# Down projection of a feed-forward layer by seven block products

## The chip, the core and the metric

One core of a Trainium2 chip runs the whole program. It has five engines with queues of their own: TensorE (PE, matmuls into PSUM; PEld is its weight load), VectorE (DVE), ScalarE (ACT), GpSimd (POOL, which does not touch PSUM here) and SyncE (SP), whose queue issues nearly all DMAs. The metric is the device time of one execution in microseconds, as the median of several.

## The reference, cut to what matters

One layer on 1024 rows of width 1024: an input projection, three groups of token mixers, an output projection with a layer norm, and then the part of this change:

```python
gu = jnp.einsum('bsd,df->bsf', x, w_gu)
gate, up = gu[..., :FFN_HIDDEN], gu[..., FFN_HIDDEN:]
ffn = jnp.einsum('bsf,fd->bsd', jax.nn.silu(gate) * up, w_down)
return layer_norm(DEEPNORM_ALPHA * x + ffn, ln2_g, ln2_b)
```

with FFN_HIDDEN = 2816, that is 22 chunks of 128, all in float32.

## The kernel before

Float32 accuracy on TensorE is had by splitting. An operand r is copied to h in the reduced format (`A.activation(h, r, AF.Copy)`, ScalarE), its rest is l = r - h (`sub(eng, l, r, f(h))`, line 158), and `mm3` (lines 180 to 182) adds the three products hh, hl, lh of 128x128 by 128x512 into one PSUM bank. The program is laid out by a planner: it orders each engine's instructions by its own forecast and puts tiles on the memory that is free, where `bufs` is the number of tiles of one tag that live at a time. So an instruction can be ahead of its place in the text, but on an engine they run strictly in the planned order. `tc.issue_after(i)` keeps a DMA behind instruction i on its queue.

*Up stage.* For each of the 22 chunks c the gate and up weights are loaded by `raws` (two tiles of tag raw, 512 KB each). Chunk 0 and 1 go plainly (`up_plain`, NPLAIN = 2); from chunk 2 on `up_strassen` uses seven products in place of eight for its own 2x2 blocks (84 matmuls): GpSimd makes four sums and differences of weight blocks (128x512 each, lines 1017 and 158), ScalarE and VectorE split them, VectorE puts the products together from PSUM and multiplies with the gate. `combos` makes the sums of the activation blocks once, while chunk 1 runs. The result th (128 hidden units by 1024 rows, of tag p with five buffers) goes to the DRAM tile `hd[c // 2][:, c % 2]` by one DMA of 512 KB in `put` (line 985), whose instruction `lead` serves later as a mark on SP's queue.

*Down stage.* Two halves hh of 512 rows, each with eight accumulators (four row tiles by two halves of the 1024 output columns), which fill all of PSUM. For each chunk `down_in` loads hidden units for 512 rows (a pair of chunks at a time) and 128 rows of `w_down`, and splits both (`split4`); `down_mm` then does 8 x 3 matmuls. The last six chunks (LASTN) are done row tile by row tile, so that the tiles end one after the other. Then VectorE adds the accumulator to 2 ALPHA x (line 1119), `layer_norm` works the statistics, and its second part scales: in mode dve on VectorE alone, in mode mix with half the columns on ScalarE and GpSimd. Each half tile is stored as it is done.

Names that matter below: `put`, `hidden`, `up_strassen`, `down_in`, `down_mm`, `layer_norm`, and the tiles th, hd, raw, y, psd.

## Time and profile before

| | us |
|---|---|
| median of three runs | 1423.05 (1419.74 to 1425.28) |
| the profiled execution | 1420.1 |
| its span in the trace | 1418.3 |
| TensorE busy in the span | 1329.7 (94%) |
| VectorE busy | 927.0 (65%) |
| ScalarE busy | 557.6 (39%) |
| GpSimd busy | 318.3 (22%) |

Busy time is a mean over stages that differ. In the first half, with attention and the selection of keys, TensorE has gaps; from about 790 us on, in the up and down stage, it has none. The busy time of a matmul in a row (0.39 us) is its latency, since matmuls are pipelined; what it costs is the distance from start to start. In a timeline row the number after the start is how long the instruction took with all that held it once it had begun, and in brackets stands how long its engine was idle before, and what ended that.

### The profile page before, as it was taken

How to read it: one execution, taken by the hardware profiler on the slowest of the kernel's cores; microseconds unless marked ns; L12 is line 12 of the kernel's file. 1: busy time of each engine (PE TensorE's matmuls, PEld its weight loads, DVE VectorE, ACT ScalarE, POOL GpSimd, SP SyncE). 2: the span in 40 equal slices, each digit the busy share in tenths (PEclk: the TensorE clock that was granted, in tenths of full speed). 3: DMA queues.
4: the chain of work that ended last, by engine and by line, in shares of the span. 5: the costliest groups of instructions: out<-in, count | busy, mean ns of one | idle time of the engine just before them, and what ended most of it. 6: DMA issues, size and time to landing. Idle time of an engine off the chain costs nothing.

```text
span 1418.3 us, 17526 instructions
## 1 busy us (share of the span) xinstructions
PE 1329.7 (94%) x6444; PEld 1065.8 (75%) x6444; DVE 927.0 (65%) x1821; ACT 557.6 (39%) x1033; POOL 318.3 (22%) x250
## 2 busy tenths in 40 slices
PE   7568987988999999899999999999999999999997
PEld 6457665676787886557788888888888888888886
DVE  5137899797657968444859776676667655348325
ACT  4145565666785534243313322222222233213310
POOL 1203221103132144400215333233333210000003
PEclk9779998899999999889999999999999999999999
DMA  6221111101111111315402222222222248427501
GB/s 192 76 74 59 49 29 43 36 9 38 51 40 41 50 34 49 96 51 182 149 33 91 86 74 90 89 79 85 90 77 75 87 182 336 149 89 269 206 0 60
DMA packets 107685, 127.46 MB, mean 90 GB/s; under 512 B 8144, under 2 KB 80720, under 8 KB 107600
## 3 DMA queue, kind: packets, MB, share of 16 engines
q1 hardware_dynamic: 106448, 122.15, 26.4%
q10 hardware_dynamic: 1152, 4.19, 0.8%
q8 instruction: 51, 0.84, 0.3%
q14 instruction: 34, 0.28, 0.1%
HBM read 97.49 MB, written 25.69 MB: 87 GB/s over the span
## 4 chain that ended last, share of the span: by engine, by line
PE 51%; DVE 1%; DMA 0%; issue 0%; ACT 0%; DVEq 0%; ACTq 0%; SPq 0%
PE p L181 9%; PE p L182 9%; PE p L180 9%; PE psd L180 6%; PE psd L182 6%; PE psd L181 6%; PE psz L182 1%; PE psz L180 1%; PE psz L181 1%; PE pg L180 1%; PE pu L182 1%; PE pu L180 1%; PE pg L182 1%; PE pg L181 1%; PE pu L181 1%; PE pst L208 0%
## 5 line engine op out<-in xcount | busy, mean ns | idle before, releaser
L559 ACT ACTIVATE junk<-sc_all,cf_a 128x768 bf16<-128x768 f32 (+2 forms) x93 | 96.7, 1039 | 35.9 <-DVE cf_a L553 14.1
L182 PE MATMUL psn<-hi_n,xTl 128*128 128x256 f32 x320 | 99.0, 309 | 0.0
L180 PE MATMUL psn<-hi_n,xTh 128*128 128x256 f32 x320 | 97.5, 305 | 0.9 <-DVE nm L664 0.9
L181 PE MATMUL psn<-lo_n,xTh 128*128 128x256 f32 x320 | 96.8, 302 | 0.0
L666 ACT ACTIVATE pt<-pt,nm 128x128 f32<-128x128 f32 (+7 forms) x96 | 74.0, 772 | 49.4 <-DVE nm L664 47.0
L198 POOL TENSOR_TENSOR lrs<-rv,mhalf 128x1 f32<-128x1 f32 x16 | 20.6, 1286 | 307.5 <-DVE rv L195 307.5
L1017 POOL TENSOR_TENSOR s<-raw_u 128x512 f32<-128x512 f32 x20 | 27.9, 1396 | 242.4 <-DMA raw_u<-in_w_gu_dram 206.9
L180 PEld LDWEIGHTS psn<-hi_n,xTh 128*128 128x128 f32 x320 | 66.2, 207 | 4.2 <-issue 2.0
L182 PEld LDWEIGHTS psn<-hi_n,xTl 128*128 128x128 f32 x320 | 66.2, 207 | 4.2 <-issue 3.0
L181 PEld LDWEIGHTS psn<-lo_n,xTh 128*128 128x128 f32 x320 | 65.8, 206 | 3.2 <-issue 1.6
L180 PE MATMUL p<-x1Th,gh 128*128 128x512 f32 x160 | 62.2, 389 | 0.0
L181 PE MATMUL p<-x1Tl,gh 128*128 128x512 f32 x160 | 62.2, 389 | 0.0
L182 PE MATMUL p<-x1Th,gl 128*128 128x512 f32 x160 | 62.2, 389 | 0.0
L365 PE MATMUL psi<-kst,qst 128*128 128x512 f32 (+1 forms) x80 | 29.0, 398 | 32.5 <-DMA qst<-qd 21.3
L372 DVE SCALAR_TENSOR_TENSOR sc_all<-rl,iw,sc_all 128x384 f32<-128x384 f32 (+5 forms) x42 | 41.4, 1046 | 27.5 <-ACT rl L367 27.4
L1043 DVE TENSOR_TENSOR th<-p,tp 128x512 f32<-128x512 f32 x20 | 13.8, 692 | 69.1 <-DMA hd<-th 57.6
L1059 ACT ACTIVATE sg<-tp 128x512 f32<-128x512 f32 x20 | 12.7, 634 | 105.6 <-DVE tp L1058 105.6
L664 DVE CUSTOM_DVE_ANT_0 pt<-psq,dist 128x512 f32<-128x512 f32 (+3 forms) x72 | 38.8, 546 | 22.0 <-PE psq L660 21.7
L198 POOL TENSOR_TENSOR rs<-rv,mhalf 128x1 f32<-128x1 f32 x32 | 19.1, 597 | 134.5 <-DVE rv L197 79.4
L1040 ACT ACTIVATE tp<-p 128x512 f32<-128x512 f32 x20 | 12.0, 600 | 93.6 <-DVE th L1065 80.4
L367 ACT ACTIVATE rl<-psi 128x512 f32<-128x512 f32 (+1 forms) x80 | 35.4, 562 | 23.7 <-PE psi L365 21.1
L682 PEld LDWEIGHTS pso<-vb,at 128*128 128x128 f32 x288 | 39.1, 206 | 7.0 <-DVE ob L705 2.4
(679 smaller groups left out, 4168.1 us busy)
## 6 DMA issues: line engine op xcount, KB each, us to landing
raw_g<-in_w_gu_dram SPq DMA_DIRECT2D x22, 512.0 KB
raw_u<-in_w_gu_dram SPq DMA_DIRECT2D x22, 512.0 KB
hd<-th SPq DMA_DIRECT2D x22, 512.0 KB
raw_n<-in_w_in_dram SPq DMA_DIRECT2D x10, 512.0 KB
x<-in_x_dram SPq DMA_DIRECT2D x8, 512.0 KB
raw_wo<-in_w_out_dram SPq DMA_DIRECT2D x8, 512.0 KB
mx<-mixd SPq DMA_DIRECT2D x8, 512.0 KB
y<-x1d SPq DMA_DIRECT2D x8, 512.0 KB
```

Source lines behind the costliest of these rows:

```text
L180: nc.tensor.matmul(ps, lh, rh, start=first, stop=False)
L181: nc.tensor.matmul(ps, lh, rl, start=False, stop=False)
L182: nc.tensor.matmul(ps, ll, rh, start=False, stop=last)
L198: GP.tensor_tensor(o, t, mhalf[:, 0:w], OP.pow)
L365: nc.tensor.matmul(ps[:, 0:w], qst[h][:, (i - 2) * P:(i - 1) * P], kst[:, o:o + w], start=True, stop=True)
L367: A.activation(r[:, o:o + w], ps[:, 0:w], AF.Relu)
L372: V.scalar_tensor_tensor(SC[i], r[:, 0:n], wcol, SC[i], op0=OP.mult, op1=OP.add)
L559: A.activation(junk_a[:, 0:P * (i + 1)], SC[i], AF.Sign, bias=f(cf)[:, j:j + 1], accum_out=cnt[:, j:j + 1])
L664: V.tensor_tensor_reduce(out=p[:, o:o + w], in0=ps[:, 0:w], in1=bias[:, o:o + w], scale=-slope, scalar=prev, op0=OP.add, op1=OP.min, accum ...
L666: A.activation(p[:, 0:n], p[:, 0:n], AF.Exp, bias=nm, scale=-1.0, accum_out=sm)
L682: nc.tensor.matmul(ps, at[:, j * P:(j + 1) * P], vsl(j0 + j), start=(j0 + j == 0), stop=(j0 + j == nk - 1))
L1017: GP.tensor_tensor(a[:, 0:4], u[:, 0:4], u[:, 4:8], OP.add)
```

## The change

Rows (two halves), hidden units (chunks j and j+11) and output columns (two halves) become the three pairs of blocks of a 2x2 by 2x2 product, which is done with seven products and sums before and after. Chunks are worked in the order 0, 11, 1, 12, ... For the first of a pair `put` keeps th (tag th, now two buffers) and stores its first half; for the second it stores th and four GpSimd results of 128x512, in two tiles of tag sh, with two more DMAs. So hd holds seven left operands per pair. The four blocks of `w_down` are loaded once each into 24 tiles (`wblock`), and GpSimd makes the differences of weights in place: t1 before product 3, one operation for each pair of chunks, t2 before product 4, three for each. A product goes over six pairs of chunks (the last a single chunk), with operands split in three buffers, into four accumulators; products alternate between the two sets of PSUM banks. Partial results stay in U, W and y, added by VectorE from PSUM and by GpSimd where both inputs are in SBUF. Seven of the eight norms are in mode mix; the first four stand in product 5, and the last product does its last three pairs row tile by row tile. The tag x8 has 13 buffers, and gl moves to the tag hi. The order of the products is 0, 1, 6, 3, 4, 5, 2.

```diff
     mixd = [dram.tile([P, DM], F32, name=f"mixd{i}") for i in range(NT)]
-    hd = [dram.tile([P, 2, S], F32, name=f"hd{i}") for i in range(NF // 2)]
+    NJ = NF // 2
+    hd = [dram.tile([P, 2, 7, 512], F32, name=f"hd{i}") for i in range((NJ + 1) // 2)]
     x1d = [dram.tile([P, DM], F32, name=f"x1d{i}") for i in range(NT)]
 
     sc_all = tl("sc", 1, "sc_all", (P, 4224))
...
         V.scalar_tensor_tensor(zz, zz, ALPHA, ps, op0=OP.mult, op1=OP.add)
 
     def x8(name, dt=F32R):
-        return pool.tile([P, 4, 512], dt, tag="x8", bufs=15, name=name)
+        return pool.tile([P, 4, 512], dt, tag="x8", bufs=13, name=name)
 
     def finish1(t):
         run(layer_norm(zs[t], g1t, b1t, EPS, "dve"))
...
     def w4(name, tag="st", bufs=11):
         return tl(tag, bufs, name, (P, KC, P), F32R)
 
+    first = {}
+
     def hidden(c):
-        return pp(f"th{c}")
+        return tl("th", 2, f"th{c}")
 
     def put(c, th):
-        return nc.sync.dma_start(hd[c // 2][:, c % 2], th).ins
+        if c < NJ:
+            first[c] = th
+            return nc.sync.dma_start(hd[c // 2][:, c % 2, 0], th[:, 0:512]).ins
+        j = c - NJ
+        d, a = hd[j // 2][:, j % 2], first.pop(j)
+        lead = nc.sync.dma_start(d[:, 1:3].rearrange("p a b -> p (a b)"), th).ins
+        u, v = tl("sh", 2, f"sa{j}"), tl("sh", 2, f"sb{j}")
+        a0, a1, b0, b1 = a[:, 0:512], a[:, 512:1024], th[:, 0:512], th[:, 512:1024]
+        GP.tensor_tensor(u[:, 0:512], a1, b1, OP.add)
+        sub(GP, u[:, 512:1024], u[:, 0:512], a0)
+        nc.sync.dma_start(d[:, 3:5].rearrange("p a b -> p (a b)"), u)
+        sub(GP, v[:, 0:512], a0, a1)
+        sub(GP, v[:, 512:1024], b0, u[:, 512:1024])
+        nc.sync.dma_start(d[:, 5:7].rearrange("p a b -> p (a b)"), v)
+        return lead
 
     def raws(c):
         r = []
...
         sub(GP, a[:, 4:8], a[:, 0:4], g[:, 0:4])
         sub(GP, b[:, 0:4], g[:, 0:4], u[:, 0:4])
         sub(GP, b[:, 4:8], g[:, 4:8], a[:, 4:8])
-        w = {"g": pair("g", g, V, w4(f"gh{c}", "hi", 3), w4(f"gl{c}", "lo", 3))}
+        w = {"g": pair("g", g, V, w4(f"gh{c}", "hi", 3), w4(f"gl{c}", "hi", 3))}
         for n, t in (("s12", a), ("s34", b)):
             w[n] = pair(n, t, V, w4(f"{n}h{c}"), w4(f"{n}l{c}"))
         uu = w4(f"uu{c}")
...
         V.tensor_tensor(h0, h0, t0, OP.mult)
         return put(c, th)
 
-    for c in range(NF):
-        if c == 1 or NPLAIN == 0 and c == 0:
+    leads = []
+    for n in range(NF):
+        c = n // 2 + n % 2 * NJ
+        if n == min(1, NPLAIN):
             T = combos()
...
+        leads.append((up_plain if n < NPLAIN else up_strassen)(c))
+
+    PAIRS = [(2 * p, min(2, NJ - 2 * p)) for p in range((NJ + 1) // 2)]
+    B = {}
+    srl = [leads[-3]]
+
+    def wblock(blk, r, d):
+        with tc.issue_after(srl[-1]):
+            for p, (j, w) in enumerate(PAIRS):
+                t = pool.tile([P, 1024], F32, tag="wd", bufs=24, name=f"B{blk}_{p}")
+                B[blk, p] = t[:, 0:512 * w].rearrange("p (a b) -> p a b", a=w)
+                src = wdn[(r + j) * P:(r + j + w) * P, d * 512:d * 512 + 512]
+                nc.sync.dma_start(B[blk, p], src.rearrange("(a p) d -> p a d", p=P))
+
+    wblock(11, 0, 0)
+
+    def split2(name, r, w):
+        h, l = (pool.tile([P, 2, 512], F32R, tag=f"{name}{e}", bufs=3, name=f"{name}{e}")[:, 0:w] for e in "hl")
         A.activation(h, r, AF.Copy)
-        sub(eng, l, r, f(h))
+        sub(V, l, r, f(h))
         return h, l
 
...
+    def operands(i, blk, p):
+        j, w = PAIRS[p]
+        r = pool.tile([P, 2, 512], F32, tag="sr", bufs=3, name="sr")[:, 0:w]
+        srl.append(nc.sync.dma_start(r, hd[p][:, 0:w, i]).ins)
+        return split2("S", r, w), split2("W", B[blk, p], w)
+
+    def product(i, blk, banks, prep, last=0):
+        acc = [al("psd") for al in banks]
+        ops = {}
+
+        def run_mm(p, t):
+            (sh, sl), (th, tl2) = ops[p]
+            j, w = PAIRS[p]
+            o = slice(t * P, t * P + P)
+            for q in range(w):
+                mm3(acc[t], sh[:, q, o], sl[:, q, o], th[:, q], tl2[:, q], j + q == 0, j + q == NJ - 1)
+
+        n = len(PAIRS)
+        for p in range(n - last):
+            prep(p)
+            ops[p] = operands(i, blk, p)
+            for t in range(4):
+                run_mm(p, t)
+        for p in range(n - last, n):
+            prep(p)
+            ops[p] = operands(i, blk, p)
+        for t in range(4):
+            for p in range(n - last, n):
+                run_mm(p, t)
+            yield t, acc[t]
 
     def store(t, ln):
         for cs in ln:
             nc.sync.dma_start(out[0, t * P:(t + 1) * P, cs], ys[t][:, cs])
 
     ys, pend = [None] * NT, []
-    with tc.issue_after(lead):
+    with tc.issue_after(leads[-1]):
         g2t, b2t = load_gb(ln2_g, ln2_b, "ln2", lambda n: tl("raw", 2, n))
...
+    setA, setB = (ps_qk, ps_qk, ps_qk, ps_av), (ps_mm, ps_mm, ps_tr, ps_tr)
+    lo_, hi_ = slice(0, 512), slice(512, 1024)
+
+    def nothing(p):
+        pass
+
+    def load_y(n):
+        ys[n] = tl("y", 8, f"y{n}")
+        with tc.issue_after(srl[-1]):
+            nc.sync.dma_start(ys[n], x1d[n])
+
+    def first_add(n, cs, ps):
+        V.scalar_tensor_tensor(ys[n][:, cs], ys[n][:, cs], 2.0 * ALPHA, ps, op0=OP.mult, op1=OP.add)
+
+    def norm(n):
+        ln = layer_norm(ys[n], g2t, b2t, 4.0 * EPS, "mix" if n < 7 else "dve", 2)
+        next(ln)
+        pend.append((n, ln))
+        if len(pend) > 1:
+            store(*pend.pop(0))
+
+    for t in range(4):
+        load_y(t)
+    U, W = (pool.tile([P, 4, 512], F32, name=n) for n in ("accu", "accw"))
+    for t, ps in product(0, 11, setA, nothing):
+        A.activation(U[:, t], ps, AF.Copy)
+        first_add(t, lo_, ps)
+    wblock(21, NJ, 0)
+    for t, ps in product(1, 21, setB, nothing):
+        V.tensor_tensor(ys[t][:, lo_], ys[t][:, lo_], ps, OP.add)
+
+    wblock(22, NJ, 1)
+
+    def t1(p):
+        sub(GP, B[11, p], B[12, p], B[11, p])
+
+    def t2(p):
+        sub(GP, B[12, p], B[22, p], B[12, p])
+        sub(GP, B[22, p], B[22, p], B[11, p])
+        sub(GP, B[21, p], B[22, p], B[21, p])
+
+    for t, ps in product(6, 22, setA, nothing):
+        first_add(t, hi_, ps)
+    wblock(12, 0, 1)
+    for t, ps in product(3, 11, setB, t1):
+        A.activation(W[:, t], ps, AF.Copy)
+        V.tensor_tensor(ys[t][:, hi_], ys[t][:, hi_], ps, OP.add)
+    for t, ps in product(4, 22, setA, t2):
+        V.tensor_tensor(U[:, t], U[:, t], ps, OP.add)
+        GP.tensor_tensor(ys[t][:, hi_], ys[t][:, hi_], U[:, t], OP.add)
+        GP.tensor_tensor(W[:, t], W[:, t], U[:, t], OP.add)
+        load_y(t + 4)
+
+    def early_norm(p):
+        if 2 <= p:
+            norm(p - 2)
+
+    for t, ps in product(5, 12, setB, early_norm):
+        first_add(t + 4, lo_, ps)
+        first_add(t + 4, hi_, ps)
+        GP.tensor_tensor(ys[t + 4][:, lo_], ys[t + 4][:, lo_], U[:, t], OP.add)
+        GP.tensor_tensor(ys[t + 4][:, hi_], ys[t + 4][:, hi_], W[:, t], OP.add)
+    for t, ps in product(2, 21, setA, nothing, last=3):
+        sub(V, ys[t + 4][:, lo_], ys[t + 4][:, lo_], ps)
+        norm(t + 4)
     for q in pend:
         store(*q)
```

## Rows read from the trace of the kernel before

**Rows 1.** Stages: stretch, length, busy us (instructions) by engine, granted clock, DMA share, GB/s.

```profile
790.50:1171.20 380.70, 380.70 (x1681) 315.23 (x1680) 259.31 (x300) 107.69 (x142) 115.31 (x76) 1.00 0.30 94
1171.20:1410.90 239.70, 239.64 (x1058) 198.09 (x1056) 111.15 (x135) 62.44 (x63) 15.13 (x13) 1.00 0.44 160
1410.90:1418.30 7.40, 0.00 (x0) 0.00 (x0) 4.37 (x8) 0.00 (x0) 0.99 (x1) 0.65 0.20 74
```

**Rows 2.** The same view, down stage, instructions on the accumulators psd alone.

```profile
1171.20:1410.90 239.70, 239.52 (x1056) 198.09 (x1056) 10.33 (x16) 1.00 0.44 160
```

**Rows 3.** Chain of work that ended last: start, us, engine, tile, line; its end.

```profile
1410.61 0.24 PE psd L182
...
1414.71 0.66 DVEq L1150
```

**Rows 4.** Timeline, GpSimd, one up-stage chunk: start, us, line, operation [idle before].

```profile
959.48 1.29 POOL L1017 TENSOR_TENSOR s<-raw_u 128x512 f32<-128x512 f32 x1 [12.02 <-DMA raw_u<-in_w_gu_dram]
960.73 1.28 POOL L158 TENSOR_TENSOR s<-raw_g,raw_u 128x512 f32<-128x512 f32 x1
...
963.78 1.62 POOL L158 TENSOR_TENSOR s<-raw_g,s 128x512 f32<-128x512 f32 x1
979.41 1.29 POOL L1017 TENSOR_TENSOR s<-raw_u 128x512 f32<-128x512 f32 x1 [14.00 <-DMA raw_u<-in_w_gu_dram]
```

**Rows 5.** Timeline of ScalarE, the copy of the sums made at 959.48.

```profile
970.75 1.05 ACT L994 ACTIVATE s12h<-s 128x1024 fp32r<-128x1024 f32 x1
```

**Rows 6.** Timeline of TensorE, first use of such a copy in that chunk.

```profile
967.32 0.39 PE L180 MATMUL p<-T1h,s12h 128*128 128x512 f32 x1
```

**Rows 7.** Timeline of VectorE in the same chunk.

```profile
964.18 0.68 DVE L1064 TENSOR_TENSOR tp<-p,tp 128x512 f32<-128x512 f32 x1
...
969.49 0.69 DVE L1043 TENSOR_TENSOR th<-p,tp 128x512 f32<-128x512 f32 x1 [3.53 <-DMA hd<-th]
```

**Rows 8.** Timeline of the SP queue in the same chunk.

```profile
975.42 0.37 SPq L162 DMA_DIRECT2D raw_u<-in_w_gu_dram  x1
```

**Rows 9.** Timeline of ScalarE, a copy of the down stage.

```profile
1162.56 1.04 ACT L1078 ACTIVATE wd_1h<-wd_1r 128x1024 fp32r<-128x1024 f32 x1
```

**Rows 10.** Timeline of VectorE, differences of the down stage.

```profile
1163.96 1.22 DVE L158 TENSOR_TENSOR wd_0l<-wd_0r,wd_0h 128x1024 fp32r<-128x1024 f32 x1
1165.10 1.22 DVE L158 TENSOR_TENSOR wd_1l<-wd_1r,wd_1h 128x1024 fp32r<-128x1024 f32 x1
```

**Rows 11.** Timeline of VectorE while GpSimd works too, 757 to 770.

```profile
757.56 2.29 DVE L158 TENSOR_TENSOR T0r<-br,x1Th 128x2048 f32<-128x2048 f32 x1
...
760.37 6.11 DVE L158 TENSOR_TENSOR T0r<-T0r,x1Tl 128x2048 f32<-128x2048 f32 x1
766.58 3.19 DVE L158 TENSOR_TENSOR T1r<-br,T0r 128x2048 f32<-128x2048 f32 x1
```

**Rows 12.** Timeline of GpSimd in the same stretch.

```profile
758.20 6.12 POOL L158 TENSOR_TENSOR T2r<-br,br 128x2048 f32<-128x2048 f32 x1 [4.83 <-ACT br L891]
764.27 3.35 POOL L1017 TENSOR_TENSOR s<-raw_u 128x512 f32<-128x512 f32 x1
767.58 3.35 POOL L158 TENSOR_TENSOR s<-raw_g,raw_u 128x512 f32<-128x512 f32 x1
```

**Rows 13.** Timeline of the SP queue: when a load was issued.

```profile
1179.97 0.62 SPq L1077 DMA_DIRECT2D wd_11r<-in_w_down_dram  x1
```

**Rows 14.** Stages view, the 40 us around the start of the down stage.

```profile
1160.00:1200.00 40.00, 40.00 (x178) 33.14 (x177) 25.77 (x28) 18.58 (x19) 0.00 (x0) 1.00 0.89 342
```

**Rows 15.** Timeline of VectorE, one norm in mode mix near the end.

```profile
1402.72 0.69 DVE L1119 SCALAR_TENSOR_TENSOR y<-y,psd 128x512 f32<-128x512 f32 x1 [2.66 <-PE psd L182]
1403.44 0.69 DVE L812 BATCH_NORM_STATS2 lst<-y 128x6 f32<-128x512 f32 x1
...
1405.74 0.75 DVE L825 SCALAR_TENSOR_TENSOR y<-y,lrs,ln2b 128x512 f32<-128x512 f32 x1
```

**Rows 16.** Timeline of GpSimd, the first multiplication of that norm.

```profile
1406.75 1.29 POOL L827 TENSOR_TENSOR y<-y,ln2g 128x512 f32<-128x512 f32 x1 [1.12 <-ACT y L824]
```

More of the change, by code (lines that the diff above doesn't have):

```diff
@@ L40 @@
 NPLAIN = 2
-LASTN = 6
 FILL_ORDER = ["v0", "b0", "b1", "b2", "v2", "b3", "vc", "c0", "g", "c1"]
@@ L1066, in up_strassen @@
         return put(c, th)
-    for c in range(NF):
-        if c == 1 or NPLAIN == 0 and c == 0:
+    leads = []
+    for n in range(NF):
+        c = n // 2 + n % 2 * NJ
+        if n == min(1, NPLAIN):
             T = combos()
-        lead = (up_plain if c < NPLAIN else up_strassen)(c)
-    def split4(name, src, hs, eng):
-        r = pp(f"{name}r")
-        h = tl("fh", 11, f"{name}h", (P, 1024), F32R)
-        l = st(f"{name}l")
-        nc.sync.dma_start(r if len(hs) == 2 else r.rearrange("p (a b) -> p a b", a=2), src)
+        leads.append((up_plain if n < NPLAIN else up_strassen)(c))
@@ L1078, in split4 @@
+    wblock(11, 0, 0)
+    def split2(name, r, w):
+        h, l = (pool.tile([P, 2, 512], F32R, tag=f"{name}{e}", bufs=3, name=f"{name}{e}")[:, 0:w] for e in "hl")
         A.activation(h, r, AF.Copy)
-        sub(eng, l, r, f(h))
+        sub(V, l, r, f(h))
         return h, l
-    def down_in(hh, c):
-        if c % 2 == 0:
-            hid[c // 2] = split4(f"hd{hh}_{c}", hd[c // 2][:, :, hh * 512:hh * 512 + 512], (P, 2, 512), V)
-        wd[c] = split4(f"wd{hh}_{c}", wdn[c * P:(c + 1) * P, :], (P, DM), V)
@@ L1087, in down_mm @@
-    def down_mm(ps, t, d, c, first, last):
-        h, l = hid[c // 2]
-        o = c % 2 * 512 + t * P
-        wh, wl = wd[c]
-        mm3(ps, h[:, o:o + P], l[:, o:o + P], wh[:, d * 512:d * 512 + 512], wl[:, d * 512:d * 512 + 512], first, last)
+    def operands(i, blk, p):
[3 more added lines that the diff above has]
+        return split2("S", r, w), split2("W", B[blk, p], w)
@@ L1097, in trunk @@
     ys, pend = [None] * NT, []
-    with tc.issue_after(lead):
+    with tc.issue_after(leads[-1]):
         g2t, b2t = load_gb(ln2_g, ln2_b, "ln2", lambda n: tl("raw", 2, n))
-    for hh in range(2):
-        hid, wd = {}, {}
-        acc = [al("psd") for al in (ps_qk, ps_qk, ps_qk, ps_av, ps_mm, ps_mm, ps_tr, ps_tr)]
-        for c in range(NF - LASTN):
-            down_in(hh, c)
-            for j in range(8):
-                down_mm(acc[j], j // 2, j % 2, c, c == 0, False)
-        for c in range(NF - LASTN, NF):
-            down_in(hh, c)
-        for t in range(4):
-            n = 4 * hh + t
-            ys[n] = tl("y", 4, f"y{n}")
-            with tc.issue_after(lead):
-                nc.sync.dma_start(ys[n], x1d[n])
-            for d in range(2):
-                ps = acc[2 * t + d]
-                for c in range(NF - LASTN, NF):
-                    down_mm(ps, t, d, c, False, c == NF - 1)
-                ds_ = slice(d * 512, d * 512 + 512)
-                V.scalar_tensor_tensor(ys[n][:, ds_], ys[n][:, ds_], 2.0 * ALPHA, ps, op0=OP.mult, op1=OP.add)
-            ln = layer_norm(ys[n], g2t, b2t, 4.0 * EPS, "mix" if 4 <= n < 7 else "dve", 2)
-            next(ln)
-            pend.append((n, ln))
-            if len(pend) > 1:
-                store(*pend.pop(0))
```

## The prediction

> **What bounds the kernel now.** I read the stage table first [rows 1]. In both the up stage (790.50 to 1171.20) and the down stage (1171.20 to 1410.90) TensorE is busy in every microsecond at a granted clock of 1.00; a cheaper product there shortens the kernel, and work of any other engine costs nothing as long as it stays ahead. In the down stage VectorE is busy for 111 of 240 us and GpSimd for 15. Next the matmuls of this stage alone [rows 2]: 1056 in 239.70 us, so one every 0.227 us. The chain's end [rows 3] says the same: matmul after matmul to 1410.9, then VectorE and the stores, 7.4 us to the end of the span. So the question is what the seven products save on TensorE, and whether their operands are still ready in time.
>
> **What goes.** Before: 2 halves x 22 chunks x 8 accumulators x 3 matmuls = 1056. After: 7 products x 11 inner chunks x 4 row tiles x 3 = 924 of the same shape. 132 x 0.227 = 30.0 us less; a product takes 29.96 us, a pair of chunks (24 matmuls) 5.45 us, the half pair at each product's end 2.72.
>
> **Up stage.** Each second chunk adds four GpSimd operations of 128x512. The row: 1.25 us from start to start without a rival [rows 4]. GpSimd works the sums of the next chunk at 959.48 to 965.4 and then waits 14 us [rows 4]; ScalarE takes them up at 970.75 [rows 5], for matmuls a chunk (84 x 0.227 = 19 us) after those of 967.32 [rows 6], at about 986. The four new ones (5 us) come when th is ready, near 966, and fit into that pause. The two th buffers make the next chunk's first write wait for the third of them, about 966 + 3.9 = 969.9; the row waits for the store of th and starts at 969.49 [rows 7]; behind it on VectorE stand the next chunk's splits, which TensorE wants more than ten us later. The two further stores per pair stand on SP's queue ahead of loads, at most some 6 us; the load of raw_u, which releases GpSimd, is asked for later still, at 975.42 [rows 8]. Price: between 0 (TensorE has no idle time to give back) and 4 us, the upper end for a queue order that delays the first operands of the down stage. I take 1.
>
> **Splits.** An operand pair costs two ScalarE copies of 1.05 us [rows 9] and two VectorE differences, 1.14 us from start to start [rows 10]. Per product that is 10 wide and 2 half-wide differences, 12.6 us of 29.96. Alone they are hidden. Operands have three buffers: the split of a pair can start when TensorE leaves the pair three before, 2 x 5.45 = 10.9 us ahead of need, and takes 1.05 + 2 x 1.14 = 3.4. The slack is 7.5 us.
>
> **The new term: one port for VectorE and GpSimd.** At 760 us both have queued work on two SBUF inputs [rows 11, 12]. VectorE's 128x2048 subtraction, 2.29 us alone at 757.56, takes 6.11 beside GpSimd's; the 128x512 on GpSimd takes 3.35 instead of 1.29; and the ends interlock, 764.3, 766.5, 767.6, 769.8: one instruction of each in turn, each waiting for the whole of the other's. An operation with a PSUM input is not held (0.68 us at 964.18, beside a GpSimd operation from 963.78) [rows 4, 7]. The change puts 24 weight differences on GpSimd around products 6, 3 and 4: 6 calls of t1, 18 of t2; of these 20 are 128x1024 and 4 are 128x512. No row has a GpSimd 128x1024 subtraction; twice the 512 one is 2.5 us, and half of T2r, which can only have begun when VectorE let go at 759.85, is 2.24. I take 2.4.
>
> The Trainium skill, page GPSIMD Engine Reference, section Elementwise — side-by-side cycle accounting, puts a two-input operation at about 2.6 cycles an element and advises VectorE for such work. As an estimate from that figure, 1024 elements take 2.2 us, and the sum below would be about 4 us better; T2r agrees with it, the 1.25 us of the 512 shape is above it.
>
> In turns, one wide difference of each engine takes 2.4 + 1.13 = 3.5 us; a pair needs two splits, 7.1 us, while TensorE eats it in 5.45. The 24 differences on GpSimd let 24 splits through (two products' worth) in 20 x 3.53 + 4 x 1.8 = 77.8 us. TensorE would use these in 59.9. Lag 17.9 less the slack of 7.5: TensorE waits 10.4 us, in pauses of one to two microseconds per pair. Lower end 0 (GpSimd's work lies in lumps that the buffers bridge), upper end 18 (no slack). I take 10.4, since both queues are full by my reading of when block B12 lands: loads are asked for far ahead (chunk 11's at 1179.97, used near 1231) [rows 13] and came at 342 GB/s in 1160 to 1200 [rows 14], so its 2.9 MB take 8.5 us.
>
> **Products 5 and 2.** VectorE has in product 5: splits 12.6, four adds into U of 0.69, four norms of about 3.4 us each (two BN_STATS of 0.69, two scaled ones of 0.75, small ones) [rows 15]: 29 us. GpSimd has eight adds and eight norm multiplications of 1.29 [rows 16], each of which can hold VectorE once: up to 20 us more. 29 to 49 against 29.96 + 7.5: a stall between 0 and 11. At the start of product 2 come eight adds from PSUM (5.5) and eight GpSimd adds: 0 to 4 more. I take 4 in all, bounds 0 and 15.
>
> **End.** Row tiles of the last product come every 15 x 0.227 = 3.4 us instead of every 8.2; VectorE needs 3.3 to 4 us for each [rows 15], and the pow and two multiplications on GpSimd 3.6. A backlog of up to some microseconds stands before the last tile, whose own chain stays at 7.4 us [rows 1]. 0 to 5, I take 2.5; less than nothing is excluded, since the last tile's chain is unchanged.
>
> Loads: 19.7 MB of left operands, 11.5 of weights, about 8 of y and output in some 210 us, 190 GB/s, below the 342 seen [rows 14]. No price.
>
> **Sum.** -30.0 + 1 + 10.4 + 4 + 2.5 = -12.1 us. The profiled execution took 1420.1 (span 1418.3 and 1.8 around it), so 1408.0; the median of the three runs is 1423.05, 2.95 above that execution, so 1411 in terms of the median. The forecast's own range is 1403 to 1417: between about 6 and 20 us of the 30 are kept.
>
> **Rivals.** (a) *All hidden.* GpSimd's differences spread so that VectorE never falls behind by 7.5 us: for it speaks VectorE's 46% share in the stage, against it the turns in [rows 11, 12]. -30 + 1 + 2.5 = -26.5: 1396.5.
>
> (b) *The saving is eaten.* The port costs its upper ends in products 3 and 4, and the norms most of theirs: -30 + 18 + 8 + 3 + 1 = 0: 1423. For it: from product 6's middle on, GpSimd's differences, adds and multiplications (some 90 us) and VectorE's two-input work (some 65) want one port for 155 of about 135 us; against it: lumps and the slack. This is also the case in which the kernel does what it says and gains nothing.
>
> (c) *GpSimd becomes the bound, and it is slower.* Place: product 4, whose weights exist only after t1 and the second differences of t2. If GpSimd takes t2 in its written order, the weights of the last pair are its 23rd operation, 76 us after its first; product 4 wants them 54 us after product 3's start. If the first slice of B12 lands s us after that start, TensorE waits 22 + s, and with 7.5 for the other terms the saving is gone at s = 0; at s = 7 the kernel is 0.5% slower, at s = 10 it takes about 1432.5. For it: B12's load is queued behind the operand reads of product 6. Against it: those reads are asked for some six pairs ahead, so I expect s near -25; and third differences, needed only by product 2, may be put last.
>
> **How the numbers follow.** Forecast 0.45, (a) 0.27, (b) 0.17, (c) 0.11. About 0.5%, 7 us, is what a measurement of this kernel can tell from no change. Faster by more: nearly all of the forecast and all of (a), 0.67. Within: the rest of the forecast and most of (b), 0.20. Slower: (c) and the worst of (b), 0.13. For 8 in 10 the range goes down to 1393, where all lower ends together lie, and up to 1427, where most of (c) and the worst of (b) are left out; all upper ends together give 1435.
>
> **What would show it.** 924 matmuls at 0.227 us in the down stage, as now but with pauses; in the up stage none. In products 6 to 4, VectorE's splits of 128x1024 at about 3.5 us instead of 1.22, GpSimd's differences at the same 3.5, and TensorE's waits ended by VectorE (rival a: waits absent; c: ended by GpSimd or by splits of product 4 that wait for GpSimd). After the last difference the splits fall back to 1.2 and the pauses stop until product 5's norms. The prediction is wrong if the pauses lie elsewhere: at the start of product 0, behind loads, or if TensorE's clock falls in the pauses below 0.77 (5.45/7.1), since then the matmuls themselves, not the splits, set the pace.

## The result: 1444.6 us, slower by 1.6%

| | before | after |
|---|---|---|
| median, us | 1422.54 | 1444.6 (1442.38 to 1447.29) |
| profiled execution; its span | 1420.1; 1418.3 | 1442.38; 1440.6 |
| first matmul of the plain chunks | 744.9 | 747.1 |
| plain chunks, to the first Strassen matmul | 45.6 | 51.2 |
| Strassen chunks | 380.8 | 394.1 |
| down stage, to the last matmul | 239.4 | 236.0 |
| from there to the end | 7.6 | 12.2 |

Each median is of four executions. The ratio is 1.0156, interval 1.0128 to 1.0184. The forecast said 1411, with a range up to 1427. The profiled executions differ by 22.3 us: +2.2 ahead of the up stage, +18.9 in it, -3.4 in the down stage, +4.6 behind it.

The stage table of the changed kernel answers to [rows 1]. Its lines are the plain chunks, the Strassen chunks, the down stage and what follows the last matmul (stretch, length, busy us and instructions of PE, PEld, DVE, ACT, POOL, granted clock, DMA share, GB/s):

```profile
747.10:798.30 51.20, 47.66 (x209) 38.60 (x208) 41.66 (x33) 19.78 (x22) 14.81 (x7) 0.97 0.23 74
798.30:1192.40 394.10, 384.07 (x1681) 315.99 (x1680) 245.18 (x301) 112.23 (x143) 160.03 (x116) 1.00 0.37 117
1192.40:1428.40 236.00, 217.38 (x925) 175.44 (x923) 168.24 (x156) 78.78 (x91) 124.59 (x61) 0.96 0.42 139
1428.40:1440.60 12.20, 0.15 (x1) 0.00 (x0) 8.49 (x15) 0.81 (x1) 6.22 (x6) 0.59 0.33 124
```

TensorE now has pauses in every stage, where [rows 1] had none, and the clock is no longer 1.00 throughout. The same view of the accumulators psd alone answers to [rows 2]:

```profile
1192.40:1428.40 236.00, 217.36 (x924) 175.44 (x923) 19.68 (x31) 4.33 (x8) 0.96 0.42 139
```

924 matmuls, as counted. At 0.227 us they need 209.7; 236.0 were spent. What each interval between the starts of successive matmuls has beyond 0.227 adds up to this. In the down stage 4.1 us lie in 1282 to 1315, 12.5 in 1315 to 1345, 1.1 to 1386, 7.4 in 1386 to 1402 (called the seam of products 5 and 2 below), 1.1 around one wait of 0.83 us at 1404, and nothing ahead of 1282; 0.1 us is rounding. The up stage has 5.9 us in 745 to 800 and 13.1 in 860 to 1030. Each has a different cause.

**Up stage, Strassen chunks.** SP's queue over one pair of chunks (start, us, queue, line, out<-in), GpSimd's last sum there and its first one behind the load, then TensorE's longest waits (in brackets: wait, and what ended it):

```profile
848.09 0.37 SPq L161 DMA_DIRECT2D raw_g<-in_w_gu_dram  x1
850.65 0.34 SPq L992 DMA_DIRECT2D hd<-th  x1
855.28 0.34 SPq L997 DMA_DIRECT2D hd<-sa  x1
856.66 0.32 SPq L1000 DMA_DIRECT2D hd<-sb  x1
857.09 0.40 SPq L161 DMA_DIRECT2D raw_u<-in_w_gu_dram  x1
...
855.33 1.30 POOL L157 TENSOR_TENSOR sb<-th,sa 128x512 f32<-128x512 f32 x1
862.44 1.28 POOL L1033 TENSOR_TENSOR s<-raw_u 128x512 f32<-128x512 f32 x1 [5.81 <-DMA raw_u<-in_w_gu_dram]
...
910.94 0.50 PE L179 MATMUL p<-bh,s34h 128*128 128x512 f32 x1 [2.45 <-DVE tp L1069]
940.82 0.50 PE L181 MATMUL p<-x1Th,gl 128*128 128x512 f32 x1 [3.03 <-DVE gl L157]
```

The load of raw_u stands right behind sb's store, which waits for GpSimd's sums. Behind raw_u come 5.3 us of transfer, four sums, the copies, the splits, gl, and the next load. This is a ring: each step waits for the one before it, and the last lets the first start again. From 857 to 960 the loads of raw_u come 18.3 to 22.8 us apart, and two successive pairs of chunks take 41.7 and 42.5 us, where twice 84 matmuls take 38.1.

**Up stage, plain chunks.** ScalarE, and the matmul that waited:

```profile
760.45 1.06 ACT L1010 ACTIVATE s12h<-s 128x1024 fp32r<-128x1024 f32 x1 [6.17 <-POOL s L157]
761.80 1.06 ACT L1010 ACTIVATE s34h<-s 128x1024 fp32r<-128x1024 f32 x1 [0.29 <-POOL s L157]
762.76 1.07 ACT L889 ACTIVATE bh<-pst 128x512 fp32r<-128x512 f32 x2
...
763.39 0.50 PE L179 MATMUL pg<-bh,gh 128*128 128x512 f32 x1 [3.31 <-ACT bh L889]
```

Copies for the first Strassen chunk wait for GpSimd's sums, and the copy that TensorE needs now (bh) stands behind them. In before the order was the other way round:

```profile
755.57 1.09 ACT L889 ACTIVATE bh<-pst 128x512 fp32r<-128x512 f32 x2 [3.45 <-PE pst L887]
...
781.55 1.04 ACT L994 ACTIVATE s12h<-s 128x1024 fp32r<-128x1024 f32 x1
```

**Products 3 and 4.** VectorE, and GpSimd's differences beside it:

```profile
1291.47 3.42 DVE L157 TENSOR_TENSOR Wl<-B,Wh 128x1024 fp32r<-128x1024 f32 x1
1294.81 3.42 DVE L157 TENSOR_TENSOR Sl<-sr,Sh 128x1024 fp32r<-128x1024 f32 x1
1298.16 3.41 DVE L157 TENSOR_TENSOR Wl<-B,Wh 128x1024 fp32r<-128x1024 f32 x1
...
1284.84 41.92 POOL L157 TENSOR_TENSOR B<-B,B 128x1024 f32<-128x1024 f32 x16
```

A split of 1.22 us [rows 10] takes 3.4 in turns with GpSimd, as the prediction had it; this costs TensorE only three pauses of 1.1 us and 0.8 us in smaller gaps. The large loss follows (ScalarE's copy, TensorE's two waits, and the stage table by 5 us):

```profile
1319.77 0.63 ACT L1107 ACTIVATE Sh<-sr 128x512 fp32r<-128x512 f32 x1 [23.08 <-POOL B L157]
...
1320.97 0.79 PE L179 MATMUL psd<-Wh,Sh 128*128 128x512 f32 x1 [7.19 <-ACT Wh L1107]
1324.32 0.79 PE L180 MATMUL psd<-Wl,Sh 128*128 128x512 f32 x1 [2.55 <-DVE Wl L157]
...
1320.00:1325.00 5.00, 1.48 (x3) 0.88 (x4) 3.83 (x2) 0.92 (x2) 5.00 (x3) 0.50 0.37 107
1325.00:1330.00 5.00, 5.00 (x16) 3.76 (x15) 3.48 (x3) 3.88 (x5) 1.68 (x2) 0.67 0.16 28
```

Sh is a copy of sr, which GpSimd never writes, yet it waited 23.08 us for GpSimd. My reading is that the planner had put its buffer on a weight slice of B11 that a second difference (B22) still had to read, and that this difference stood in GpSimd's queue behind four third ones (B21). No view shows the addresses; e8_third below bears on it. After a wait of 7.19 us the granted clock was 0.50, that is 1.2 GHz; matmuls started 0.43 us apart until 1328.3, and from 1329 the clock was 1.00.

**Product 5 into product 2.** VectorE, ScalarE, TensorE:

```profile
1372.69 0.16 DVE L823 SCALAR_TENSOR_TENSOR lnb<-lmv,lrs 128x1 f32<-128x1 f32 x1 [4.06 <-POOL lrs L197]
...
1389.58 0.74 DVE L825 SCALAR_TENSOR_TENSOR y<-y,lrs,ln2b 128x512 f32<-128x512 f32 x1
1391.49 1.45 DVE L157 TENSOR_TENSOR Sl<-sr,Sh 128x1024 fp32r<-128x1024 f32 x1 [1.17 <-ACT Sh L1107]
...
1389.70 0.81 ACT L824 ACTIVATE y<-y,lnb,lrs 128x512 f32<-128x512 f32 x1 [3.98 <-DVE lnb L823]
1390.42 1.04 ACT L1107 ACTIVATE Sh<-sr 128x1024 fp32r<-128x1024 f32 x1
...
1392.46 0.50 PE L179 MATMUL psd<-Wh,Sh 128*128 128x512 f32 x1 [2.32 <-ACT Wh L1107]
1395.20 0.80 PE L180 MATMUL psd<-Wl,Sh 128*128 128x512 f32 x1 [2.24 <-DVE Wl L157]
```

Norm 3 goes first on both engines, the first split of product 2 after it.

**End.** VectorE takes up the four last tiles 4.2 to 4.8 us apart, from the second on each straight behind the norm before it (compare [rows 15], where it waited 2.66 us for TensorE):

```profile
1418.39 0.69 DVE L157 TENSOR_TENSOR y<-y,psd 128x512 f32<-128x512 f32 x1 [2.33 <-PE psd L181]
...
1422.54 0.68 DVE L157 TENSOR_TENSOR y<-y,psd 128x512 f32<-128x512 f32 x1
...
1427.29 0.68 DVE L157 TENSOR_TENSOR y<-y,psd 128x512 f32<-128x512 f32 x1
...
1431.99 0.68 DVE L157 TENSOR_TENSOR y<-y,psd 128x512 f32<-128x512 f32 x1
```

### The profile page after: what moved, and what is told of

It is laid out like the page before. It is cut to its first block, busy times and chain, and to the rows that moved or that the text cites. A ratio compares the mean times of both kernels' runs of the same rounds, so it can differ in the third digit from the quotient of the medians.

```text
span 1440.6 us, 17530 instructions
## 1 busy us (share of the span) xinstructions
PE 1312.9 (91%) x6312; PEld 1044.2 (72%) x6312; DVE 971.9 (67%) x1851; ACT 579.8 (40%) x1063; POOL 469.4 (33%) x342
## 4 chain that ended last, share of the span: by engine, by line
PE 28%; POOL 9%; DVE 6%; DMA 4%; issue 3%; ACT 2%; SPq 0%; DVEq 0%; POOLq 0%; ACTq 0%
PE p L181 5%; PE p L180 5%; PE p L179 5%; DMA raw_u<-in_w_gu_dram 3%; POOL B L157 3%; PE psd L180 3%; PE psd L181 3%; PE psd L179 3%; POOL s L157 2%; PE psz L179 1%; PE psz L180 1%; PE psz L181 1%; POOL s L1033 1%; ACT s12h L1010 1%; DVE gl L157 1%
## 5 line engine op out<-in xcount | busy, mean ns | idle before, releaser
L180 PE MATMUL psd<-Wl,Sh 128*128 128x512 f32 x308 | 122.9, 399 | 9.1 <-DVE Wl L157 9.0
L179 PE MATMUL psd<-Wh,Sh 128*128 128x512 f32 x308 | 121.6, 395 | 9.5 <-ACT Wh L1107 9.5
L181 PE MATMUL psd<-Wh,Sl 128*128 128x512 f32 x308 | 121.5, 395 | 0.0
L157 DVE TENSOR_TENSOR Sl<-sr,Sh 128x1024 fp32r<-128x1024 f32 (+1 forms) x42 | 67.0, 1594 | 52.4 <-ACT Sh L1107 48.7
L1107 ACT ACTIVATE Sh<-sr 128x1024 fp32r<-128x1024 f32 (+1 forms) x42 | 41.4, 986 | 114.6 <-PE psd L180 60.7
L157 POOL TENSOR_TENSOR B<-B,B 128x1024 f32<-128x1024 f32 (+1 forms) x24 | 65.6, 2767 | 60.8 <-DMA B<-in_w_down_dram 60.7
L180 PEld LDWEIGHTS psd<-Wl,Sh 128*128 128x128 f32 x308 | 58.8, 191 | 25.6 <-DVE Wl L157 13.4
L179 PEld LDWEIGHTS psd<-Wh,Sh 128*128 128x128 f32 x308 | 58.9, 191 | 22.9 <-ACT Wh L1107 10.4
L157 DVE TENSOR_TENSOR Wl<-B,Wh 128x1024 fp32r<-128x1024 f32 (+1 forms) x42 | 69.0, 1643 | 1.3 <-ACT tp L1056 1.1
L181 PEld LDWEIGHTS psd<-Wh,Sl 128*128 128x128 f32 x308 | 58.8, 191 | 11.9
```

Source lines behind the costliest of these rows:

```text
L157: eng.tensor_tensor(o, a, b, OP.subtract)
L179: nc.tensor.matmul(ps, lh, rh, start=first, stop=False)
L180: nc.tensor.matmul(ps, lh, rl, start=False, stop=False)
L181: nc.tensor.matmul(ps, ll, rh, start=False, stop=last)
```

## The experiments

In these kernels the first matmul of the up stage comes anywhere from 739 to 753 us, since every edit lets the planner order the stages ahead of it anew. Stage lengths are therefore compared, not totals. Each experiment but the last is a single execution. A stage can repeat closely (the Strassen part took 394.1 us in the changed kernel and in e2_act, the down stage 236.0 to 236.2 in the changed kernel, e6_put and e18_bh), but the planner can also shift one that an edit did not touch: see e24_op.

### Up stage

**Stores of the sums on another queue** (`e6_put`), and beforehand **operands read late** (`e1_late`).

```
e6:  -  nc.sync.dma_start(d[:, 3:5]..., u)      and the same for d[:, 5:7], v
     +  A.dma_start(d[:, 3:5]..., u)
e1:  +  with tc.issue_after(srl[0]):            around the load of sr in operands
```

> All reads of left operands are held on SP's queue behind the store of chunk n = 19 (one line in operands); before, the planner put the six reads of product 0 into the up stage, from 918 us on, where the first three splits hold their buffers for up to 270 us. In the changed kernel the up stage takes 445.1 us (747.1 to 1192.2) against 426.3 before, the down stage 236.3, the rest after the last matmul 12.1. Theory Q (SP's order and the memory that early operands hold delay the raw loads of the up stage): up stage down to 432 to 440. Rival P (the four sums on GpSimd hold the port against VectorE): up stage stays at 443 to 447, since no sum is moved. Down stage unchanged by both, 234 to 239.

> The two stores of GpSimd's sums in put are issued on ScalarE's queue in place of SP's. Theory Q (raw_u's load stands on SP behind these stores, which wait for the sums: 850 to 857 us in the changed kernel): the up stage comes down from 445.1 to 434 to 440. Rival P (the port): 443 to 447. A third way: ScalarE now waits for the sums with its splits behind, and the stage grows over 447. Down stage 234 to 239.

e1 made the Strassen part 405.8 us, 11.7 longer, outside what either theory had: the early reads of operands were not the cause. e6:

```profile
801.50:1182.30 380.80, 380.80 (x1681) 315.32 (x1681) 248.37 (x301) 110.68 (x141) 163.55 (x116) 1.00 0.36 120
```

All 13.3 us are gone, with GpSimd's sums still there (163.55 us busy, 115.31 in [rows 1]). In the pair shown above raw_u was issued 6.4 us behind the store of th (850.65, 857.09); in e6 it is 2.3 us (849.79, 852.06). The cause was the place of two stores in SP's queue, not the work. Of e1 the trace tells this much: in the changed kernel the order on SP's queue changes from 939 on (both stores stand ahead of raw_g, no longer between raw_g and raw_u), and TensorE loses nothing after 1030; in e1 every pair to the end of the stage has raw_u right behind sb's store, the loads come 22.8 to 24.3 and 18.0 to 18.6 us apart in turn, and TensorE waits until 1158. Why the planner kept this order there is open.

**The two buffer sizes alone, in the kernel before** (`e15_bufs`): x8 13 for 15, gl with gh.

> The kernel before with two sizes of the change alone: 13 buffers in place of 15 for the tiles of 4 blocks x 512, and the lower half of g in the buffers of the upper halves. Nothing is left out. Theory S: the 5.6 us that the changed kernel loses in the two plain chunks come from these buffers, which were given up to make room: 45.6 becomes 50 to 52 us and the whole 1422 to 1428. Rival O: they come from the new order of the chunks and from the sums that GpSimd makes behind the second one: the plain chunks stay at 45 to 47 us and the whole within 2 us of the kernel before.

```profile
745.30:790.70 45.40, 45.40 (x210) 37.64 (x209) 43.61 (x33) 19.43 (x22) 20.78 (x6) 1.00 0.24 77
```

No loss: theory S falls.

**The copies held behind bh** (`e18_bh`, on e6):

```
 A.activation(bh...)            ->  last_bh.append(A.activation(bh...).ins)
 w = {"g": ...}; s12, s34       ->  with tc.issue_after(last_bh[-1]): the same
```

> As the run e6_put (plain chunks 50.9, Strassen part 380.8, span 1430.6 us), with one order on ScalarE changed: the copies of the first Strassen chunk's combinations (s12h, s34h) are held behind the last copy of bh. Nothing is left out. Theory Q2: the 5 us of the plain part are those two copies, which the new order of chunks has brought ahead of bh in ScalarE's queue (762.24 and 763.58, bh only at 764.55 where TensorE waits for it 3.19 us, then slow clock), and which wait there for a load and for GpSimd. Held behind, the plain part is 45 to 47 us and the span 1424 to 1427. Rival: the first Strassen chunk then gets its halves too late: plain 45 to 47, Strassen part 384 to 387, span 1429 to 1432.

Plain chunks 45.8, so Q2 holds for them. But the Strassen part became 387.5, later and in another place than the rival had it:

```profile
1005.18 0.50 PE L181 MATMUL p<-x1Th,gl 128*128 128x512 f32 x1 [3.98 <-DVE gl L157]
```

In e8_third, with the same edit of the stores but the plain loss unmended, this gl ended 260.0 us after the first matmul of the plain chunks, here 260.6, but there TensorE was 5 us further behind and did not wait for it. The 5 us lost early had hidden the 6 us lost here.

**Operands read late, once more, on the mended kernel** (`e24_op`; its base e23_nh2 is below):

> As e23_nh2, but no operand of the products is read before the store of the third last chunk's result stands in SP's queue. Nothing is left out. Theory E: the 4 to 6 us lost near 1004 (TensorE waits 3.57 us for gl) come from the early read and split of product 0's first operand, whose split Sl stands at VectorE ahead of gl; without it the Strassen part falls from some 386 to 381 to 383 us, and the down stage grows by 0 to 3 us. Rival F: they come from put's sums, which hold the memory that s12l waits for (VectorE 2.43 us behind sb): Strassen part 385 us or more.

```profile
790.00:1170.80 380.80, 380.80 (x1682) 315.31 (x1681) 240.29 (x301) 110.83 (x141) 165.69 (x116) 1.00 0.36 118
```

380.8 against 385.7: theory E. The planner alone moved this part, too: in the six runs with e18's order of the copies and operands read early (e18, e16, e17, e20, e23, e26) it took 382.7 to 389.0 us. But in e24, as in f1_best with the same edit, TensorE waits for no gl and loses nothing in it. With three orders mended the up stage (426.5) is that of before (426.4), sums and all.

### Products 3 and 4

**Differences left out** (`e3_nodiff`, t1 and t2 empty; products 3, 4, 5 and 2 then use the plain blocks).

> The weight differences t1 and t2 are left out, so products 2 to 5 use the plain blocks; all else is as in the changed kernel. There, TensorE loses 4.1 us in 1282 to 1315 in pauses of about 1.1 per pair and 12.5 in 1315 to 1345, one long wait and a slow clock behind it. Theory M (the long wait is a split that takes memory of block B11, which the late second differences still read; the short ones are the port): both go, down stage 236.3 - 16.6 = 218 to 222. Rival L (the prediction's sum, the port alone at 10.4): 224 to 228. Up stage 445 by both.

```profile
1182.80:1402.00 219.20, 213.08 (x925) 174.59 (x923) 139.60 (x156) 79.00 (x91) 59.04 (x37) 0.98 0.44 149
```

Of 236.0 us 16.8 were GpSimd's differences; the seam of product 5 and 2 stayed at 7.4.

**Third differences last** (`e8_third`, on e6):

```
 last2 = GP.tensor_tensor(B[22, p], B[22, p], B[11, p], OP.subtract)
 if p == len(PAIRS) - 1:
     with tc.issue_after(last2.ins):
         for k in range(p + 1): sub(GP, B[21, k], B[22, k], B[21, k])
```

> The changed kernel with the stores of the sums on ScalarE's queue (as in the run e6_put: span 1430.6, down stage 236.1 us) and, besides, the six third weight differences (B21) held on GpSimd behind the last second difference (B22). Nothing is left out; GpSimd does the same work in another order. Theory M: the 12.5 us lost between 1315 and 1345 come from memory that is held. A split of product 3's last pair lies on a B11 slice, and the second difference that reads this slice last stands in GpSimd's queue behind four third differences (4 x 3.0 us). Moved ahead of them it ends some 12 us sooner, and the wait of 7.34 us with the slow clock behind it goes: 0 to 4 us are left of the 12.5, down stage 225 to 229 us, span 1419 to 1423. Rival P: the loss is the sum of GpSimd's work and of the turns that it takes with VectorE, and their order is of no weight: down stage 234 to 238 us.

```profile
1293.19 1.06 ACT L1107 ACTIVATE Sh<-sr 128x1024 fp32r<-128x1024 f32 x1 [13.83 <-POOL B L1187]
```

231.7: between the two theories. The losses between 1270 and 1325 fell from 16.8 us in e6 to 12.3, the longest wait from 5.75 to 3.36 us. The order counts, as M has it. What is left is in large part of the same kind: TensorE's waits are ended by VectorE's splits, but 9.2 us of the loss come behind copies of Sh that ScalarE could start only when a GpSimd difference had ended, at 1293.19 right behind a second one (here they have a line of their own, L1187), at 1305.71 after 3.49 us. Only the pauses of 1.2 us are splits in turns alone, as P has it.

**Two of three differences on VectorE** (`e17_dv`, on e16_fix below): `sub(V, ...)` for B11 and B12.

> As e16_fix, with the first two of the three weight differences of each pair on VectorE (1.2 us each) and only B22's and B21's on GpSimd. Nothing is left out. Theory G: what is left in products 3 and 4 (10.4 us in e8_third, waits for Wl of 0.96 to 3.36 us) comes from GpSimd working without a pause from 1250 to 1314, one turn for each of VectorE's splits. With half of the differences it stops sooner, and 2 to 6 us are left: down stage 4 to 8 us below e16_fix. Rival W: the eleven differences more on VectorE, at up to 3.4 us in turns, make its splits later: down stage 0 to 8 us above e16_fix.

```profile
1175.50:1400.90 225.40, 214.27 (x925) 173.86 (x924) 170.35 (x168) 79.77 (x92) 97.64 (x49) 0.98 0.44 148
```

225.4, 8.2 below e16_fix; products 3 and 4 lose 4.9 us there instead of 13.1. Theory G. VectorE at 1.2 us a difference costs less than GpSimd, whose differences hold up its splits in turns (3.4 us each in the same run).

### Product 5 into product 2

**Stores of the early norms on ScalarE's queue** (`e2_act`): `(A if t < 4 else nc.sync).dma_start(out...)`.

> The stores of row tiles 0 to 3 are issued on ScalarE's queue in place of SP's. In the changed kernel TensorE loses 7.4 us between 1386 and 1430, where the reads for product 2 stand behind stores that wait for GpSimd's multiplications. Theory Q: these 7.4 us shrink to 0 to 2 and the down stage to 229 to 232. Rival N (VectorE is overloaded by the norms, my prediction's term for products 5 and 2): the loss stays at 5 to 8, down stage 234 to 238. Up stage 445 by both.

```profile
1390.06 0.81 ACT L824 ACTIVATE y<-y,lnb,lrs 128x512 f32<-128x512 f32 x1 [4.14 <-POOL y L828]
```

The seam lost 8.3 us, not less than 7.4, and the down stage took 239.2, longer than either theory had it. This does not clear the stores: on ScalarE's queue they stand ahead of the same copies, and the norm at 1390.06, with the first split's copy behind it, waited 4.14 us for a y of GpSimd (L828) that the store ahead of it needed. The changed kernel's own trace does: three reads for product 2 were issued by 1386.00, and ScalarE copies Sh at 1390.42 straight behind norm 3, without waiting for a transfer.

**Norms 0 to 3 left out** (`e9_nonorm`, on e6; their rows are stored at the end as they are).

> As the run e6_put (down stage 236.1, tail 12.2 us), but the normalisations of row tiles 0 to 3 in product 5 are left out; these rows are stored at the very end as they are. Theory N: the 7.4 us lost between 1386 and 1430 come from these four normalisations, which stand in VectorE's and ScalarE's queues ahead of the splits and wait there for GpSimd's power, itself behind GpSimd's eight additions. Without them 0 to 2 us are left of the 7.4: down stage 228 to 231 us. The 12.5 us of product 4 stay, and the tail stays at 12 to 13 us. Rival: the loss comes from the eight first additions behind product 5's matmuls or from the late read of product 2's operands: down stage 235 to 237 us.

```profile
1365.00:1400.00 35.00, 33.72 (x149) 27.63 (x148) 27.45 (x24) 11.79 (x14) 16.83 (x10) 1.00 0.27 98
```

Down stage 229.1; one wait of 1.28 us is left at the seam, and the clock stays 1.00. The norms are the cause. The tail stays at 12.4.

**U and W added by VectorE** (`e13_av`, on e8): the sixteen `GP.tensor_tensor` as `V.tensor_tensor`.

> As the run e8_third, but the sixteen additions of the partial results U and W (GpSimd, 128x512) are made by VectorE. Nothing is left out. Theory N, its second half: what makes the normalisations late is the power behind eight of these additions on GpSimd (1357.8 to 1372 in the changed kernel). With the additions on VectorE (about 0.7 us each, 11 us over two products) the 7.4 us fall to 0 to 3: down stage 218 to 225 us, 4 to 7 below e8_third. Rival: VectorE's own queue is what is late there, and 11 us more on it make it later: down stage 2 to 6 us above e8_third.

```profile
1389.01 0.80 PE L180 MATMUL psd<-Wl,Sh 128*128 128x512 f32 x1 [8.22 <-DVE Wl L157]
```

The wait for the power disappeared, and the seam got no better (down stage 232.6): eight more additions now stood ahead of product 2's splits. My half-theory, that the power (lrs) behind GpSimd's additions was what mattered, fell.

**Splits asked for earlier** (`e16_fix`: e8 and e18, plus):

```
 product(5, ...): norm(p - 3) behind the operands of pair p >= 3, not norm(p - 2) ahead of them
 at its end, ahead of first_add:  ahead[0] = operands(2, 21, 0)
 norm(3) behind product 2's second pair
```

> As e8_third (down stage 231.7, span 1425.4 us), with the order of e18_bh on ScalarE, and in product 5: the splits of product 2's first pair asked for ahead of the eight first additions of product 5, and each of the normalisations 0 to 3 emitted one pair later and behind the splits. Nothing is left out. Theory N in its new form: the 7.5 us lost at 1369 to 1389 are an order of VectorE's queue (norm, then first additions, then the splits that TensorE waits for); with the splits ahead 0 to 2 us are left: down stage 223 to 227 us, span 1411 to 1417. Rival V: VectorE has too much to do there in any order: down stage 229 to 233 us.

233.6, seam 8.8: rival V by the number. The Strassen part took 389.0 us here, with a wait of 3.50 us for gl as in e18, which the expectation did not have. But the trace of e17_dv, with the same edit, shows norm 3 at 1361.36 on ScalarE and the first split's copy at 1362.08 behind it: the order in which the program asks is not the order that the planner writes. So the hold was made explicit (`e23_nh2`, on e17):

```
 vsp.append(V.tensor_tensor(l, r, f(h), OP.subtract).ins)          in split2
 with tc.issue_after(vsp[-1]):  around norm(p - 3), norm(3) and product 5's first_add
 ahead for two pairs
```

> As e17_dv (span 1413.1, down stage 225.4 us, of which 8.7 are lost where product 5 passes into product 2), but the splits of product 2's first two pairs are asked for ahead, and the normalisations 0 to 3 and the first additions of product 5 are held on VectorE behind the split that was asked for last. Nothing is left out. Theory N: the loss is the place of the normalisations in VectorE's and ScalarE's queues, ahead of the splits (the planner had put them there in e16_fix and e17_dv too: 1361.36 the norm, 1362.08 the first split). Held behind, 0 to 2 us are left: down stage 217 to 220 us, span 1404 to 1408. Rival V: VectorE's total work there is too much: the loss stays at 5 us or more, or comes back within product 2: down stage 222 us or more.

223.8: only 1.6 less. The wait moved to product 2's third pair, whose split stood behind the eight first additions, the end of norm 2 and the start of norm 3 (4.90 us in e23 and e24).

### The end

**Four pairs kept for the row tiles** (`e20_l4`, on e16; `e26_l4`, on e23): own buffers for product 2's last pairs, `last=4`.

> As e16_fix, but product 2 ends with four pairs of chunks kept for its row tiles (7 chunks, 21 matmuls, 4.77 us a tile at the trace's 0.227) in place of three (5 chunks, 3.41 us). Nothing is left out. Theory T: the tail of 12.2 us comes from four normalisations of some 4.5 us each in a row on VectorE behind tiles that come every 3.4 us; with 4.77 us between tiles only the last one is left: tail 8 to 10 us, down stage 0 to 2 us longer, the whole 1 to 4 us below e16_fix. Rival: the tail stays at 11.5 to 12.5 (it is GpSimd's part of the norms), or the four pairs are split too late and the down stage grows by 3 us or more: the whole 0 to 4 us above e16_fix.

> As e23_nh2, with four pairs kept for the row tiles of product 2 as in e20_l4 (tail 8.2 us there, but 29 us lost in products 3 and 4). Nothing is left out. Theory M: that loss was memory: the larger set of buffers of product 2 lay on weight slices and moved the splits of products 3 and 4 behind GpSimd's differences. With two of the three differences on VectorE the slices come free sooner: the loss is 0 to 8 us, tail 8 to 9 us, span 2 to 4 us below e23_nh2 in the better case. Rival: the loss does not hang on GpSimd's differences: 15 us or more, span 10 us or more above e23_nh2.

```profile
1446.30:1454.50 8.20, 0.13 (x1) 0.00 (x0) 4.78 (x8) 0.00 (x0) 3.39 (x3) 0.67 0.34 128
...
1299.93 1.06 ACT L1110 ACTIVATE Wh<-B 128x1024 fp32r<-128x1024 f32 x1 [36.17 <-POOL B L157]
...
1305.23 0.79 PE L179 MATMUL psd<-Wh,Sh 128*128 128x512 f32 x1 [28.73 <-ACT Wh L1110]
```

The tail is 8.2 (9.0 in e26): the distance of the tiles is its cause, theory T. The price was 37 us lost in product 3 (16 in e26), and not for memory, as I had expected for e26: in the order of ScalarE's queue these copies of Wh are product 2's, of pairs 2 to 5. Having free buffers, the planner placed them among those of product 3, where they wait for GpSimd's third differences and everything behind them waits too.

### All together

`f1_best`: e24 with norm 3 behind product 2's last split.

> As e24_op (span 1407.1, down stage 224.1, tail 12.2 us), but normalisation 3, and with it the second half of normalisation 2, is emitted behind product 2's last split and not behind its second. Nothing is left out. Theory N: the 7.9 us lost at 1364 to 1384 (TensorE waits 4.90 us for Wl, then slow clock) come from these two standing ahead of the third pair's split on VectorE; without them 0 to 3 us are left: down stage 217 to 220 us, tail 12 to 14, span 1400 to 1404, the whole 0.982 to 0.990 of the kernel before. Rival: VectorE is late there in any case, the loss stays at 5 us or more or goes over to the tail (15 us or more): span 1406 or more, 0.990 or more of the kernel before.

```profile
743.40:789.20 45.80, 45.61 (x210) 37.56 (x209) 42.99 (x33) 19.42 (x22) 14.10 (x6) 1.00 0.22 73
789.20:1170.00 380.80, 380.80 (x1682) 315.42 (x1681) 241.50 (x301) 110.51 (x141) 165.49 (x116) 1.00 0.36 119
1170.00:1387.00 217.00, 211.84 (x925) 172.54 (x923) 169.39 (x161) 78.86 (x91) 92.92 (x45) 1.00 0.46 153
1387.00:1405.40 18.40, 0.17 (x1) 0.00 (x0) 13.64 (x22) 2.12 (x3) 10.76 (x9) 0.60 0.35 129
```

Median 1408.51 us of four executions, 0.9897 of the kernel before (interval 0.9868 to 0.9925), 36 us below the changed kernel. Products 5 and 2 lose 3.2 us now, the down stage is 7.3 us above the 209.7 of its matmuls. But the rival's second half came true: norms 3 to 7 now stand in a row on VectorE, 4.3 us apart, and the tail is 18.4 us. VectorE's norms cost some 6 to 7 us either at the seam or at the end (down stage 7.1 us shorter than in e24, tail 6.2 longer). Whether they fit anywhere else was not tried.

## Why the prediction was wrong

The forecast was 1411, the range ended at 1427, and 1444.6 was measured. The terms, in its order:

1. **-30.0 for the matmuls.** Right: 924 of them, at 0.227 us wherever they ran freely.
2. **Up stage, +1 in 0 to 4.** It was +18.9, and this is the step that failed. The prediction looked at the time of raw_u's load in before ("asked for later still", 975.42, [rows 8]) and took it for its place in the queue. With the stores of sa and sb there it stands behind them: they wait for GpSimd, and raw_u releases GpSimd, so a store's wait was put into the ring that feeds the next chunk. The delay itself ("at most some 6 us") was of the right size, 4.1 us in the pair shown (6.4 less 2.3); that the load had time to spare was not right. e6_put gave back its 13.3 us. The other 5.6 (5.1 from e6_put to e18_bh), the order of ScalarE's copies in the plain chunks, were in no step; I had costed GpSimd's time and queues, but not that a planner may put a waiting copy ahead of a needed one.
3. **Port, +10.4 in 0 to 18.** The mechanism was as described: 3.5 us predicted for a turn, 3.35 from start to start. The size was not: its direct price was 4.1 us. The sum let 24 splits go in turns without a break; in the trace 14 did (1264.2 to 1308.2), and then VectorE had no copy to split for 12.21 us, because of item 4. A GpSimd difference takes 4.61 / 2 = 2.3 us where VectorE leaves it alone (two at 1293.12 in e8_third), 2.4 was taken. The Trainium skill, page GPSIMD Engine Reference, section Elementwise — side-by-side cycle accounting, gives some 2.6 cycles an element; the estimate of 2.2 us from it agrees with this. Its advice to use VectorE for such work agrees with e17_dv, 8.2 us.
4. **Products 3 and 4, another 12.5 us.** Rival (c) named the culprit, GpSimd, and nearly the place (it had product 4; the wait was for the last pair of product 3), but set its condition by data: it needs B12's first slice s = 0 us or more after product 3's start. The first difference began at 1261.0, product 3 at 1282.3, so s is about -21, near the -25 that it expected, and by data there was no loss. By my reading it came through memory (Sh on a slice of B11) and through third differences ahead of second ones, which (c) expected last. e3_nodiff shows that GpSimd's differences cost this, e8_third that their order counts; that the wait was for memory rests on what Sh reads and on what its copies wait for in both traces, not on a view of the addresses.
5. **Products 5 and 2, +4 in 0 to 15.** 7.4 at the seam and 2.2 in smaller waits (1.1 at 1376 to 1382, 1.1 at 1404), so 9.6, within the bounds. The sum was of work; what decided was the place of norm 3 ahead of a split (e9_nonorm, e23_nh2, f1_best).
6. **End, +2.5 in 0 to 5.** 4.6, within the bounds, and by the mechanism named (e20_l4).

So the terms other than the up stage were right or within their bounds (products 3 and 4 with 4.1 + 12.5 = 16.6 in 0 to 18, though by luck: three quarters of it came for another reason), and the sign was still wrong: the up stage, priced at 1 us with 4 as its upper end, took 18.9. It was not the only miss. Every term that was not exact came out above its middle: with the others as measured (16.6 + 9.6 + 4.6) and the up stage at 1, the sum is -30.0 + 31.8, no gain, near rival (b) and close to the upper end of the range. The up stage's 18.9 carried the kernel out of the range and, beyond noise, to slower. Two signs that the prediction had given for being wrong both came: pauses outside products 6 to 4, and a clock in the pauses below 0.77 (0.50 after 1320.97). The page of before did show the order of the SP queue; what it could not show was the order that the planner would choose for the changed program.

## What to carry to other kernels

When a change adds a store that waits for a slow engine, ask what stands behind it in that queue and whether the slow engine itself waits for that: a ring is priced by its whole length, not by the store's 0.3 us. Where an engine's queue is ordered by a planner, the price of a step is set less by its work than by what it is put ahead of; two stores on another queue, a handful of orders held by hand, and two of three differences on another engine turned +1.6% into -1.0% with not one matmul changed. A stage that loses time early can hide a loss later, so mending one wait needs a look at the next.
